# Two edits to the order of work in a hybrid attention and SSM block: the scaled x paced by weight units, and three small pieces of the scan put at one place

## The chip, the cores and the metric

The kernel runs on one core of a Trainium2 chip. The metric is the device time of one execution in microseconds (us). The kernel before took 1399.06 us, the median of three runs from 1398.83 to 1401.26.

A core has engines that run side by side, each with its own queue of instructions in a fixed order: TensorE (PE in the profile; its weight loads are PEld), VectorE (DVE), ScalarE (ACT), GpSimd (POOL) and SyncE (SP, which here only starts transfers). They wait for each other through semaphores. An instruction that waits holds up all that stands behind it on its engine.

## The reference

One layer of a block with 256 tokens and width 2048, all in fp32. What matters here:

```python
hn = rms_norm(x, norm_w)
proj = hn @ w_in                      # 2048 x 20544 columns
q, k, v, z_a, z_s, xbc, dt_raw, g_a, g_s = split(proj)
o_a = mixed_dilated_attention(q, k, v) * silu(z_a)
xs, bm, cm = split(silu(causal_depthwise_conv(xbc)))
dt = softplus(dt_raw + dt_bias); acum = cumsum(dt * a) within chunks of 128
cb = C @ B^T                          # per group and chunk
y = (cb * decay) @ (xs * dt) + carried state + d_skip * xs
y = rms_norm(y * silu(z_s), ssm_norm_w)
merged = sigmoid(g_a) * (o_a @ w_attn) + sigmoid(g_s) * (y @ w_ssm)
return rms_norm(x + merged @ w_out, final_norm_w)
```

The SSM part has 8 groups. A group has a block B and a block C of 128 columns and four blocks of 128 columns each of xs and z_s (8 heads of 64).

## The kernel before, in words

**Products in fp32.** Each operand of a product is kept as a high part h and a low part l, both of a shorter type that TensorE takes at a higher rate, and a product is three products (h by h, l by h, h by l). All weights are streamed once, in units of 128 partitions by 1024 numbers (`unit`, L210 to L222): SP starts the transfer of unit n into w, ScalarE writes h (L221) and VectorE writes l = w - h (L222). There are four buffers each for w, h and l, so unit n can be split once TensorE is done with unit n - 4. The units stand in one order for the whole kernel: first a mixed block (unit 0 to 7), dt (unit 8), the gates gs 0 and 1 (units 9 to 24), then the groups.

**The start.** The first block and the gates gs 0 and 1 are computed from x without its row norm, as split in yT[0], and the norm is multiplied in behind. All that follows takes x with the norm, kept split in XT. `find_r` (L717) computes the norm of each row and spreads it over the partitions: rb_x on TensorE (L481), and a copy rx on VectorE (L717) that lies in the tile `early`. `norm_x(c)`, for c from 0 to 7, takes two of the 16 blocks of x: one multiplication by rx over 128x512 (L530), and for each block the split, h on ScalarE (L229) and l on VectorE (L233). The first product that reads XT is xs of block 1, right behind the gates. Also waiting for rx are the first step of dt (L561), a multiplication of the three raw conv inputs (L606) and one of z_s (L721).

**A projection.** B, C, each xs and each zs are one projection each (`gemm_a`): 2 units, 32 matmuls, in turn one with h (128x512, L260) and one with l (128x256, L261).

**The SSM pieces of a group.** Beside its ten projections, a group g has three pieces on TensorE:

- C B (`make_cb`): two matmuls "cbp" (L617, L618) into a bank of PSUM called m1, then a multiplication by the mask on VectorE (L619).
- the turning of x (`turn`): eight transposes "xtp" (L650) into two banks m1, then two multiplications by dt on VectorE (L653). There are two m1 banks in all.
- the scan (`scan`): 32 matmuls "yp" (L668) of 64 columns each into the m2 banks, then on VectorE and ScalarE the work on y: L678, L681, the squares L682, the sums ssq L683, and the split into yT (L229, L233). Of the last group yT is needed by the product that follows the groups, ssm.

The scan needs `decays`: for each of four pairs of heads a transfer acb (256 KB, L626, one buffer) from acum, which dt has written to memory (L583), six ScalarE instructions (L631, L635), and per two pairs an exponential (L639) and a multiplication by C B on VectorE (L640). The bias of these comes from `dt_turn` (TensorE transposes dt_tp L591, and lastb L595).

**What sets the order.** Each projection calls `tick()` once, a gate product once per two units. `after(t, f)` puts f on a list to be written t ticks later. `on_unit[n]` is called when unit n has been split. This gives the order in which the program is written; from it a scheduler puts the instructions into the queues of the engines, with the splitting of units 120 places ahead.

Of the kernel before, what the change touches and what calls it, by code (L numbers as in the profile page):

```python
# [9 lines left out]
F32 = mybir.dt.float32  # L10
F32R = mybir.dt.float32r
AF = mybir.ActivationFunctionType
ALU = mybir.AluOpType
PSUM = bass.MemoryType.PSUM

P = 128
S = 256
# [4 lines left out]
SH = 64  # L22
# [10 lines left out]
X_CUTS = ((0, 1), (1, 2), (2, 4), (4, 6), (6, 8), (8, 10))  # L33
N_FINE = 4
N_ACT_X = 1
DT_LAG, CB_LAG, TURN_LAG, GT_LAG, Y_LAG, S_LAG, M_LAG = 2, 3, 2, 2, 11, 2, 2
GS_BEFORE = {0: (0, 1), 4: (2,)}
NEG = -1.0e30
S_QUADS = {
    ("ssm", 0): (5, 7, 9, 11, 13), ("ssm", 2): (3, 5, 7, 9, 11, 13),  # L40
# [14 lines left out]
def weight_plan():  # L55
# [5 lines left out]
    def rows(tag, src, off, n_kt):  # L61
        plan.append((tag, "b", src, off, n_kt, 512))
# [6 lines left out]
    for g in range(GROUPS):  # L69
        for c in GS_BEFORE.get(g, ()):  # L70
            rows(("gs", c), "w_in", OFF_GS + c * 512, KT)
# [78 lines left out]
def constants():  # L150
# [7 lines left out]
    count = m1.astype(np.float32) + m2 + m3  # L158
    cst[:, 0:384] = np.where(count > 0, -dist, NEG)
    cst[:, 384:768] = count  # L160
# [11 lines left out]
def hybrid_block(ctx: ExitStack, tc: tile.TileContext, wall, xt, x, pk_d, cst_d, fw_d, out):  # L172
    nc = tc.nc
    ve, ac, gp, pe = nc.vector, nc.scalar, nc.gpsimd, nc.tensor
# [29 lines left out]
    on_unit = {}  # L204
# [23 lines left out]
    def split(src, hi, lo, scale=1.0):  # L228
        ac.activation(hi, src, AF.Copy, scale=scale)  # L229
        if isinstance(scale, float):  # L230
            ve.tensor_tensor(lo, src, hi.bitcast(F32), ALU.subtract)
        else:
            ve.scalar_tensor_tensor(lo, src, scale, hi.bitcast(F32), ALU.mult, ALU.subtract)  # L233
# [4 lines left out]
    def after(ticks, f):  # L238
        due.append((now[0] + ticks, f))
# [78 lines left out]
    def half_silu(h, out_ap, name):  # L318
        th = ev.tile([P, S], F32, name=f"th_{name}", tag="th", bufs=2)
        ac.activation(th, h, AF.Tanh)  # L320
        ve.scalar_tensor_tensor(out_ap, th, 1.0, h, ALU.add, ALU.mult)
# [140 lines left out]
    def gates(tag, th, src, scales=(0.5, 0.5)):  # L462
        accs = gemm_b(tag, lambda kt: src[:, kt, :])
        for i in range(2):
            ac.activation(th[:, i, tag[1] * 512 : tag[1] * 512 + 512], accs[i], AF.Tanh, scale=scales[i])
# [20 lines left out]
    xr, dts, rx = early[:, :KT, :], early[:SH, KT:28, :], early[:, 28, :]  # L486
# [19 lines left out]
    def fetch(dst, src, behind):  # L506
        gp.tensor_copy(dst[:, 0:1], behind)
        nc.sync.dma_start(dst, src)
# [16 lines left out]
    on_unit[10] = lambda behind: fetch(cst[:, 1152:], cst_d[:, 1152:], behind)  # L525
    on_unit[13] = lambda behind: fetch(cst[:, :1152], cst_d[:, :1152], behind)

    def norm_x(c):
        cs = slice(2 * c, 2 * c + 2)
        ve.tensor_tensor(xr[:, cs], xr[:, cs], rx.unsqueeze(1).to_broadcast([P, 2, S]), ALU.mult)  # L530
        for kt in range(2 * c, 2 * c + 2):
            split(xr[:, kt], XT[:, kt, :S], XT[:, kt, S:], scale=pk[:, kt : kt + 1])

# [2 lines left out]
    with tc.tile_pool(name="ssm", bufs=2) as sp:  # L536
        ev = sp
        for tag in ("lo", "eh", "th"):
            sp.tile([P, S], F32, name=f"first_{tag}", tag=tag, bufs=2)
        dtT = sp.tile([P, 2, SH], F32, name="dtT", tag="dtT", bufs=1)  # L540
        acT = sp.tile([P, 2, SH], F32, name="acT", tag="acT", bufs=1)
        crT = sp.tile([P, SH], F32, name="crT", tag="crT", bufs=1)
# [10 lines left out]
        def dt_chain():  # L553
            used = []

            def tmp():
                used.append(0)
                return dts[:, len(used) - 1, :]

            raw, neg, e, z, s, pl, lo, dt, da, ac_t, one = (tmp() for _ in range(11))  # L560
            ve.tensor_tensor(raw, lo, rx[:SH], ALU.mult)  # L561
            ve.tensor_scalar(raw, raw, pk[:SH, 320:321], None, ALU.add)
            ve.scalar_tensor_tensor(neg, raw, -1.0, raw, ALU.mult, ALU.max)
            ac.activation(e, neg, AF.Exp, scale=-1.0)
            ve.tensor_scalar(s, e, 2.0, None, ALU.add)
            ve.reciprocal(z, s)
            ve.tensor_tensor(z, z, e, ALU.mult)
            ve.tensor_tensor(s, z, z, ALU.mult)
            ve.tensor_scalar(pl, s, 1.0 / 17.0, 1.0 / 15.0, ALU.mult, ALU.add)
            for n in (13, 11, 9, 7, 5, 3, 1):  # L570
                ve.tensor_tensor(pl, pl, s, ALU.mult)
                ve.tensor_scalar(pl, pl, 1.0 / n, None, ALU.add)
            ve.tensor_tensor(pl, pl, z, ALU.mult)
            ve.tensor_scalar(pl, pl, 2.0, None, ALU.mult)
            ve.tensor_scalar(raw, raw, 0.0, None, ALU.max)
            ve.tensor_tensor(dt, pl, raw, ALU.add)
            ac.activation(a_neg, pk[:SH, 321:322], AF.Exp)
            ve.tensor_scalar(da, dt, a_neg, -1.0, ALU.mult, ALU.mult)
            gp.memset(one, 1.0)
            for c in range(2):  # L580
                cs = slice(c * P, (c + 1) * P)
                ve.tensor_tensor_scan(ac_t[:, cs], one[:, cs], da[:, cs], 0.0, ALU.mult, ALU.add)
            nc.sync.dma_start(acum_d, ac_t)  # L583
            after(DT_LAG, lambda: dt_turn(dt, ac_t))

        def dt_turn(dt, ac_t):
            tp = bank("m1", 2, "dt_tp")
            for i, src in enumerate((dt, ac_t)):
                for c in range(2):
                    o = (2 * i + c) * SH  # L590
                    pe.transpose(tp[:, o : o + SH], src[:, c * P : (c + 1) * P], ident[:SH, :SH])  # L591
            ve.tensor_copy(dtT, tp[:, 0:128].rearrange("p (c h) -> p c h", c=2))
            ve.tensor_copy(acT, tp[:, 128:256].rearrange("p (c h) -> p c h", c=2))
            lastb = bank("m2", 2, "lastb")
            pe.matmul(lastb[:, :SH], sel, acT[:, 0], start=True, stop=True)  # L595
            ve.tensor_tensor(crT, lastb[:, :SH], acT[:, 0], ALU.subtract)
# [6 lines left out]

        def conv(raw, ct, out_ap, name, late=False):
            if late:
                ve.tensor_tensor(raw[:, 4:], raw[:, 4:], rx, ALU.mult)  # L606
            h = ev.tile([P, S], F32, name=f"cv_{name}", tag="eh", bufs=2)
            ac.activation(h, raw[:, 4:], AF.Identity, scale=cw[:, 144 + ct : 145 + ct], bias=cw[:, 192 + ct : 193 + ct])
            for k in range(3):
                ve.scalar_tensor_tensor(  # L610
                    h, raw[:, 1 + k : 1 + k + S], cw[:, 48 * k + ct : 48 * k + ct + 1], h, ALU.mult, ALU.add
                )
            half_silu(h, out_ap, name)

        def make_cb(g, bt, ct_, cb):
            p = bank("m1", 2, f"cbp{g}")
            pe.matmul(p[:, :S], bt[:, :P], ct_, start=True, stop=True)  # L617
            pe.matmul(p[:, S : S + P], bt[:, P:], ct_[:, P:], start=True, stop=True)  # L618
            ve.tensor_tensor(cb, p[:, :384], mask3, ALU.mult)  # L619
# [85 lines left out]
        zh0 = first["zs"][:, 0]  # L705
# [12 lines left out]
            ve.tensor_scalar(cw, pk[:, 16:256], 0.5, None, ALU.mult)  # L718

        def finish_z0():  # L720
            ve.tensor_tensor(zh0, zh0, rx, ALU.mult)  # L721
            half_silu(zh0, zh0, "z0")

        after(2, find_r)
        for c in range(8):
            after(3 + c * 6 // 8, lambda c=c: norm_x(c))
        for ticks, f in (
            (8, dt_chain),
            (9, lambda: conv(raws[0], 32, group[0], "B0", True)),
            (9, lambda: conv(raws[1], 40, group[1], "C0", True)),  # L730
            (10, lambda: conv(raws[2], 0, first["xs"][:, 0], "x0", True)),
            (10, finish_z0),
            (11, lambda: make_cb(0, *group)),
        ):
            after(ticks, f)
        for c in GS_BEFORE[0]:
            gates(("gs", c), th_s, yT[0], hr_x)

        for g in range(GROUPS):
            if g:  # L740
                for c in GS_BEFORE.get(g, ()):
                    gates(("gs", c), th_s, XT)
# [6 lines left out]
            for t in range(max(4 * g, 1), 4 * g + 4):  # L749
                u, i = divmod(t, 2)  # L750
# [3 lines left out]
                if t % 4 == 3:  # L754
                    after(TURN_LAG, lambda a=(g, state): turn(*a))

                    y_lag = Y_LAG + 4 * len(GS_BEFORE.get(g + 1, ()))
                    for k in range(4):
# [144 lines left out]
    with tc.tile_pool(name="fin", bufs=2) as fp:  # L903
# [40 lines left out]
        for c0 in (0, 2):  # L944
# [8 lines left out]
            for i in range(2):  # L953
                f = fs[:, i, :8]
                for c, acc in zip((c0, c0 + 1), es[2 * i : 2 * i + 2]):
                    cs = slice(c * 512, (c + 1) * 512)
# [11 lines left out]
        for i in range(2):  # L968
            r = fs[:, i, 7:8]
            for c in range(4):  # L970
                cs = slice(c * 512, (c + 1) * 512)
# [40 lines left out]
```

## Time and profile before

| | |
|---|---|
| median of three runs | 1399.06 us (1398.83 to 1401.26) |
| the profiled execution's own time | 1398.06 us |
| its span, first to last instruction | 1396.3 us |
| granted TensorE clock, mean | 0.998 |
| TensorE busy | 1383.9 us (99%) |
| VectorE busy | 1088.8 us (78%) |
| ScalarE busy | 810.2 us (58%) |
| GpSimd busy | 18.7 us (1%) |
| instructions | 19873 |
| memory traffic | 194 GB/s over the span |

The profiled execution is 1.0 us under the median, and 1.8 us of it lie outside the span. The trace models the end of a matmul and lets neighbours overlap, so the duration of a row is longer than the distance to the next; the time that a stretch of TensorE takes is read from the starts. All times in what follows are microseconds from the first instruction of the profiled execution.

### The profile page before, as it was taken

The page shows a single profiled execution, that of the slowest core. Times are in us where ns is not written, and L with a number is a line of the kernel's source. Part 1 is how long each engine was busy: PE and PEld are TensorE (multiplying, and loading weights), DVE is VectorE, ACT ScalarE, POOL GpSimd, SP SyncE. Part 2 cuts the span into 40 slices and gives each one's busy share as a digit, 9 for nine tenths or more (in the row PEclk, how much of TensorE's full clock was granted, in tenths as well). Part 3 has the DMA queues.
Part 4 walks back from the last instruction along what each step waited for, and adds up shares of the span by engine and source line. Part 5 has one row for each costly group of instructions (what it writes and reads, how often), then busy time and mean ns, then how long its engine had stood idle before and what let it go on. Part 6 is the DMA issues. An engine that isn't in the chain of part 4 may idle for free.

```text
span 1396.3 us, 19873 instructions
## 1 busy us (share of the span) xinstructions
PE 1383.9 (99%) x7308; PEld 1178.1 (84%) x7308; DVE 1088.8 (78%) x1622; ACT 810.2 (58%) x1258; POOL 18.7 (1%) x72
## 2 busy tenths in 40 slices
PE   9999999999999999999999999999999999999997
PEld 8788888888888888888888888888888888888886
DVE  6988787786788787798988988666666766487887
ACT  7657577675667575665554555545454454454554
POOL 1000000000000000000000000000000000000000
PEclk9999999999999999999999999999999999999999
DMA  8666665666565665556666565655555555667564
GB/s 333 217 205 207 184 204 170 213 183 205 175 204 180 208 188 185 181 175 212 190 221 196 193 215 183 211 179 170 176 169 180 176 172 172 204 211 245 175 199 136
DMA packets 78210, 272.33 MB, mean 195 GB/s; under 512 B 8800, under 2 KB 9376, under 8 KB 77728
## 3 DMA queue, kind: packets, MB, share of 16 engines
q1 hardware_dynamic: 77392, 269.88, 61.4%
q8 instruction: 57, 0.93, 0.3%
q10 hardware_dynamic: 720, 1.18, 0.2%
q14 instruction: 41, 0.34, 0.1%
HBM read 268.86 MB, written 2.16 MB: 194 GB/s over the span
## 4 chain that ended last, share of the span: by engine, by line
PE 97%; DVE 2%; DMA 0%; issue 0%; ACT 0%; SPq 0%; POOL 0%; POOLq 0%; DVEq 0%
PE ps_zs L260 8%; PE ps_xs L260 8%; PE ps_k L260 4%; PE ps_za L260 4%; PE ps_q L260 4%; PE ps_zs L261 4%; PE ps_xs L261 4%; PE ps_ssm L377 3%; PE ps_ssm L379 3%; PE ps_ssm L378 3%; PE ps_q L261 2%; PE ps_za L261 2%; PE ps_k L261 2%; PE ps_B L260 2%; PE ps_C L260 2%; PE ps_gs L337 2%
## 5 line engine op out<-in xcount | busy, mean ns | idle before, releaser
L222 DVE TENSOR_TENSOR l<-w,h 128x1024 fp32r<-128x1024 f32 (+1 forms) x432 | 522.0, 1212 | 222.7 <-ACT h L221 219.9
L221 ACT ACTIVATE h<-w 128x1024 fp32r<-128x1024 f32 (+1 forms) x432 | 452.0, 1050 | 417.1 <-issue 98.4
L260 PE MATMUL ps_zs<-XT,h 128*128 128x512 f32 x496 | 175.7, 396 | 0.0
L260 PE MATMUL ps_xs<-XT,h 128*128 128x512 f32 x496 | 174.5, 393 | 0.0
L261 PE MATMUL ps_zs<-XT,l 128*128 128x256 f32 x496 | 139.5, 281 | 0.0
L261 PE MATMUL ps_xs<-XT,l 128*128 128x256 f32 x496 | 139.1, 280 | 0.0
L260 PEld LDWEIGHTS ps_zs<-XT,h 128*128 128x128 f32 x496 | 93.0, 187 | 22.1 <-issue 1.2
L260 PEld LDWEIGHTS ps_xs<-XT,h 128*128 128x128 f32 x496 | 92.9, 187 | 20.9
L261 PEld LDWEIGHTS ps_zs<-XT,l 128*128 128x128 f32 x496 | 93.7, 189 | 0.1
L261 PEld LDWEIGHTS ps_xs<-XT,l 128*128 128x128 f32 x496 | 93.7, 189 | 0.0
L260 PE MATMUL ps_q<-XT,h 128*128 128x512 f32 x256 | 92.4, 404 | 0.0
L260 PE MATMUL ps_za<-XT,h 128*128 128x512 f32 x256 | 89.7, 394 | 0.0
L260 PE MATMUL ps_k<-XT,h 128*128 128x512 f32 x256 | 89.7, 394 | 0.0
L261 PE MATMUL ps_q<-XT,l 128*128 128x256 f32 x256 | 71.3, 278 | 0.0
L261 PE MATMUL ps_k<-XT,l 128*128 128x256 f32 x256 | 71.0, 278 | 0.0
L261 PE MATMUL ps_za<-XT,l 128*128 128x256 f32 x256 | 71.0, 278 | 0.0
L378 PE MATMUL ps_ssm<-l,yT 128*128 128x512 f32 x168 | 65.2, 389 | 0.0
L379 PE MATMUL ps_ssm<-h,yT 128*128 128x512 f32 x168 | 65.2, 390 | 0.0
L377 PE MATMUL ps_ssm<-h,yT 128*128 128x512 f32 x168 | 57.5, 390 | 0.0
L260 PEld LDWEIGHTS ps_k<-XT,h 128*128 128x128 f32 x256 | 48.0, 188 | 11.3
L260 PEld LDWEIGHTS ps_za<-XT,h 128*128 128x128 f32 x256 | 48.0, 188 | 11.3
L260 PEld LDWEIGHTS ps_q<-XT,h 128*128 128x128 f32 x256 | 48.1, 188 | 10.9
(517 smaller groups left out, 2963.7 us busy)
## 6 DMA issues: line engine op xcount, KB each, us to landing
w<-in_wall SPq DMA_DIRECT2D x480, 512.0 KB, 3.7
acb<-acum_d SPq DMA_DIRECT2D x32, 256.0 KB, 3.6
th_s<-in_x SPq DMA_DIRECT2D x4, 512.0 KB, 7.1
vth<-in_x SPq DMA_DIRECT2D x1, 2048.0 KB, 9.4
early<-in_xt SPq DMA_DIRECT2D x7, 256.0 KB, 6.8
fw<-in_fw SPq DMA_DIRECT2D x1, 1024.0 KB, 6.0
out<-vth SPq DMA_DIRECT2D x4, 256.0 KB, 2.9
out<-vth ACTq DMA_DIRECT2D x4, 256.0 KB, 3.2
```

The source lines that it names most:

```text
L221: ac.activation(h[:, a:b], w[:, a:b], AF.Copy)
L222: ve.tensor_tensor(l[:, a:b], w[:, a:b], h[:, a:b].bitcast(F32), ALU.subtract)
L260: pe.matmul(acc, h[:, kk, :], m, start=(kt == 0), stop=False)
L261: pe.matmul(acc[:, S:], l[:, kk, :], m[:, :S], start=False, stop=(kt == KT - 1))
L337: pe.matmul(accs[i], xh, l[:, kk], start=False, stop=False)
L377: pe.matmul(acc, xh, h, start=start, stop=False)
L378: pe.matmul(acc, xh, l, start=False, stop=False)
L379: pe.matmul(acc, xl, h, start=False, stop=stop)
```

## The change

**Scaled x.** `norm_x(0)` still takes rx itself, three ticks on. For c from 1 to 7, `norm_x(c)` is now written when unit 16 + c has been split (units 17 to 23, one block each). Ahead of it GpSimd makes a copy of rx for this c, in a new tile rxs that shares the memory of the tile gt: it first copies one column of the unit's h into the place (128x1), which makes it wait for that unit, and then rx (128x256). The multiplication of `norm_x(c)` reads that copy, and so waits for the unit. The other readers of rx (dt, the raw conv inputs, z_s) read the last copy, and dt is due one tick later.

**SSM pieces.** The lags of the list change, in ticks: C B from 3 to 9.5, the turning of x from 2 to 3, decays from 2 to 3, the scan from 11 to 13. A group has ten ticks; with these numbers the C B of group g, the scan of group g - 1 and the turning of x of group g are due at the same place, between B and C of group g + 1.

The number of instructions on TensorE, VectorE and ScalarE is the same but for the grouping; GpSimd has 14 more.

```diff
-DT_LAG, CB_LAG, TURN_LAG, GT_LAG, Y_LAG, S_LAG, M_LAG = 2, 3, 2, 2, 11, 2, 2
+DT_LAG, CB_LAG, TURN_LAG, GT_LAG, Y_LAG, S_LAG, M_LAG = 2, 9.5, 3, 3, 13, 2, 2
 GS_BEFORE = {0: (0, 1), 4: (2,)}
+RX_UNITS = {c: 16 + c for c in range(1, 8)}
...
+    rx_of = {}
+
+    def later_rx(n):
+        def copy(behind):
+            rx_of[n] = rxs[:, n]
+            gp.tensor_copy(rx_of[n][:, 0:1], behind)
+            gp.tensor_copy(rx_of[n], rx)
+        return copy
+
     def norm_x(c):
         cs = slice(2 * c, 2 * c + 2)
-        ve.tensor_tensor(xr[:, cs], xr[:, cs], rx.unsqueeze(1).to_broadcast([P, 2, S]), ALU.mult)
+        r = rx_of.get(c, rx)
+        ve.tensor_tensor(xr[:, cs], xr[:, cs], r.unsqueeze(1).to_broadcast([P, 2, S]), ALU.mult)
...
+        rxs = sp.tile([P, 12, S], F32, name="rxs", tag="gt", bufs=1)
...
-            ve.tensor_tensor(raw, lo, rx[:SH], ALU.mult)
+            ve.tensor_tensor(raw, lo, rx_of[7][:SH], ALU.mult)
...
-                ve.tensor_tensor(raw[:, 4:], raw[:, 4:], rx, ALU.mult)
+                ve.tensor_tensor(raw[:, 4:], raw[:, 4:], rx_of[7], ALU.mult)
...
-            ve.tensor_tensor(zh0, zh0, rx, ALU.mult)
+            ve.tensor_tensor(zh0, zh0, rx_of[7], ALU.mult)
...
-        for c in range(8):
-            after(3 + c * 6 // 8, lambda c=c: norm_x(c))
+        after(3, lambda: norm_x(0))
+        for c, u in RX_UNITS.items():
+            on_unit[u] = lambda behind, c=c: (later_rx(c)(behind), norm_x(c))
         for ticks, f in (
-            (8, dt_chain),
+            (9, dt_chain),
```

Below, rows of the queues as the two programs have them: line, operation, result <- operands, with the number of the unit or block in the name, and x for the same row several times. The lines of the changed program are 1 to 14 higher than those of the kernel before.

VectorE at the start, before. The first row is the copy rx, "early" on the left of a TENSOR_TENSOR of 128x512 is a `norm_x` multiplication, XT the l part of a split block of x, l16 to l18 the l parts of the weight units of gs 1.

```order
L717 COPY early_80<-rb_x_450 128x256
L530 TENSOR_TENSOR early_80<-early_80 128x512 x8
L561 TENSOR_TENSOR early_80<-early_80 64x256
L606 TENSOR_TENSOR raw_first0_348<-raw_first0_348,early_80 128x256
L606 TENSOR_TENSOR raw_first1_353<-raw_first1_353,early_80 128x256
L606 TENSOR_TENSOR raw_first2_358<-raw_first2_358,early_80 128x256
L721 TENSOR_TENSOR zs0_364<-zs0_364,early_80 128x256
L222 TENSOR_TENSOR l16_565<-w16_562,h16_564 128x1024
L233 SCALAR_TENSOR_TENSOR XT_77<-early_80,pk_72,XT_77 128x256 x8
L222 TENSOR_TENSOR l17_592<-w17_589,h17_591 128x1024
```

The same place after:

```order
L730 COPY early_80<-rb_x_451 128x256
L542 TENSOR_TENSOR early_80<-early_80 128x512
L223 TENSOR_TENSOR l16_556<-w16_553,h16_555 128x1024
L234 SCALAR_TENSOR_TENSOR XT_77<-early_80,pk_72,XT_77 128x256 x2
L223 TENSOR_TENSOR l17_578<-w17_575,h17_577 128x1024
L542 TENSOR_TENSOR early_80<-early_80,rxs_114 128x512
L223 TENSOR_TENSOR l18_603<-w18_600,h18_602 128x1024
```

One multiplication, not eight, stands ahead of l16; the others follow one to a unit, each behind the l of its unit, and the multiplications for dt, the raw inputs and z_s stand behind l23.

TensorE in a steady group, before: the scan of group 1 (yp1) between an xs and a zs, then the transposes of group 2 (xtp2) four matmuls ahead of the end of B of group 3, then C B of group 3 (cbp3) inside a zs.

```order
L668 MATMUL yp1_0_2385<-gt1_1836,xdt1_1823 64x128 x2
L260 MATMUL ps_zs11_2423<-XT_77,h75_2426 128x512
...
L261 MATMUL ps_B3_2500<-XT_77,l78_2526 128x256
L650 MATMUL xtp2_1_2480<-cst_78,xs5_2250 128x128 x4
L650 MATMUL xtp2_0_2479<-cst_78,xs4_2024 128x128 x4
L260 MATMUL ps_B3_2500<-XT_77,h78_2525 128x512
...
L617 MATMUL cbp3_2746<-ct3_2476,bt3_2475 128x256
L618 MATMUL cbp3_2746<-ct3_2476,bt3_2475 128x128
L261 MATMUL ps_zs13_2808<-XT_77,l87_2812 128x256
```

After, between B and C of group 3 (the rows of yp1 that repeat left out):

```order
L262 MATMUL ps_B3_2451<-XT_77,l78_2477 128x256
L630 MATMUL cbp2_2509<-ct2_1794,bt2_1793 128x256
L631 MATMUL cbp2_2509<-ct2_1794,bt2_1793 128x128
L681 MATMUL yp1_1_2514<-gt1_1909,xdt1_1896 64x256 x2
L681 MATMUL yp1_1_2514<-gt1_1909,xdt1_1896 64x128 x2
...
L681 MATMUL yp1_0_2513<-gt1_1909,xdt1_1896 64x128 x2
L663 MATMUL xtp2_1_2553<-cst_78,xs5_2261 128x128 x4
L663 MATMUL xtp2_0_2552<-cst_78,xs4_2031 128x128 x4
L261 MATMUL ps_C3_2573<-XT_77,h79_2576 128x512
```

All three pieces stand in one row, and a matmul with h follows.

TensorE at the end of the groups, before: the scan of group 7 (yp7) begins inside the last gate product, gs 3, is broken by ten of its matmuls, and ends ahead of ssm.

```order
L668 MATMUL yp7_1_6098<-gt7_5914,xdt7_5901 64x256
L337 MATMUL ps_gs3_0_5899<-l192_6070,XT_77 128x512
L338 MATMUL ps_gs3_0_5899<-h192_6069,XT_77 128x512
```

After, inside ssm:

```order
L380 MATMUL ps_ssm0_3_6216<-h195_6255,yT0_81 128x512
L681 MATMUL yp7_1_6113<-gt7_5965,xdt7_5952 64x256 x2
L681 MATMUL yp7_1_6113<-gt7_5965,xdt7_5952 64x128 x2
...
L681 MATMUL yp7_0_6112<-gt7_5965,xdt7_5952 64x128 x2
L378 MATMUL ps_ssm0_0_6213<-h196_6261,yT0_81 128x512
```

The scan of group 7 is whole again and stands 36 matmuls into ssm.

## The prediction

> **What bounds the kernel now.** I read the page first, then the waits of TensorE, the chain, and the timeline where the change works. The page:
>
> ```profile
> PE 1383.9 (99%) x7308; PEld 1178.1 (84%) x7308; DVE 1088.8 (78%) x1622; ACT 810.2 (58%) x1258; POOL 18.7 (1%) x72
> ...
> PE 97%; DVE 2%; DMA 0%; issue 0%; ACT 0%; SPq 0%; POOL 0%; POOLq 0%; DVEq 0%
> ```
>
> TensorE is busy for 99% of the span and holds 97% of the chain; 2% belongs to VectorE. So the change can gain in two ways only: a wait of TensorE goes, or the same matmuls run in less time. The waits:
>
> ```profile
> PE ps_gs L337 <- DVE l L222: 1.7, 2, 1.2
> PE warm L492 <- DVE ssq L489: 1.4, 1, 1.4
> PE ps_first L306 <- ACT h L221: 0.2, 1, 0.2
> ```
>
> Only the first lies where the change works: two waits of the gate product for an l. The chain shows what is late there (start, duration):
>
> ```profile
> 43.67 0.76 DVE early L530 x2
> 44.43 0.45 issue
> 44.88 3.70 DVE early L530 x6
> ...
> 50.25 1.14 DVE l L222
> 51.38 2.05 DVE XT L233 x6
> ...
> 54.56 1.13 DVE l L222
> ...
> 58.73 1.15 DVE l L222
> 59.92 0.50 PE ps_gs L337
> 62.49 0.45 PE ps_gs L336 x2
> 65.21 0.45 PE ps_gs L336 x2
> ```
>
> From 43.67 on VectorE does the eight multiplications of norm_x in one go (0.62 each), and splits of x ahead of l17 and l18, for which TensorE then waits. The last two rows are one weight unit apart: 2.72 us. In the timeline the two late matmuls stand as
>
> ```profile
> 55.75 0.50 PE L337 MATMUL ps_gs<-l,yT 128*128 128x512 f32 x1 [0.55 <-DVE l L222]
> 59.92 0.50 PE L337 MATMUL ps_gs<-l,yT 128*128 128x512 f32 x1 [1.15 <-DVE l L222]
> ```
>
> 0.55 + 1.15 = 1.7 us of waiting. Behind each wait TensorE also has to start up again, so by the starts of all matmuls there the two cost about 2.0 us.
>
> **Scaled x: what it removes.** With one multiplication ahead of l16, VectorE's run is 0.62 (norm_x 0), 1.14 (l16), two splits 0.68 (2.05 / 6 each), 1.14 (l17) from 43.67: l17 is there at 47.3, where the first of the two waits shows that it is wanted at 55.2. Lead 7.9 us. Each further unit then asks VectorE for 1.14 + 0.68 + 0.62 = 2.44 us against 2.72 of TensorE. Ahead of l24 also stand the multiplications for dt, the raw inputs and z_s, 1.7 us (the chain's gap between the last norm_x, 48.58, and l16, 50.25). So both stalls go: **-2.0 us**, unless the copies cost what the next paragraph bounds. It cannot be more, since TensorE waits for nothing else there.
>
> **Scaled x: what it adds.** Seven copies of 128x1 and seven of 128x256 on GpSimd, and a wait of seven multiplications for them. No 128x256 copy on GpSimd is in the trace. The nearest rows are one-column copies:
>
> ```profile
> 29.74 1.24 POOL L507 COPY cst<-h 128x1 f32<-128x1 f32 x1 [3.25 <-ACT h L221]
> 38.90 0.18 POOL L507 COPY cst<-h 128x1 f32<-128x1 f32 x1 [0.30 <-ACT h L221]
> ```
>
> The same copy takes 0.18 or 1.24 us. The long one starts with an l of VectorE, which the same h releases, and lasts as long as that l does. So a GpSimd copy can be held by a VectorE instruction; whether VectorE is held too these rows do not say. Per unit, what the multiplication waits, w, lies between 0 (the first copy hides beside the l, the second beside the two splits) and 2.48 (both take 1.24, nothing hides them). Slack of l24: 7.9 + 7 x (2.72 - 2.44) - 1.7 - 7w = 8.2 - 7w, and never more than some 4.7, since h23 can be written only when unit 19 has been used. VectorE stalls TensorE again from w = 1.2. I take w = 0.3 (a short second copy that falls between two splits), and **+0.3 us** for what ScalarE, which has the same splits to do, may be late with; ends 0 and 9.2 (7 x 2.48 - 8.2).
>
> A page of the Trainium skill speaks against the change here. "SBUF — State Buffer", section "Who interferes with whom", says that VectorE and GpSimd share a pair of ports as an exclusive lock, that an instruction of VectorE with two operands in SBUF contends with a GpSimd instruction that reads SBUF, and that the loser is blocked for the whole instruction. The trace agrees with the half that it shows (1.24 against 0.18 us); that VectorE loses as well no row shows.
>
> The last rx copy now comes behind unit 23, so dt starts some 20 us later, and its result too. The first C B, decays and dt_turn of group 0 follow. Group 0 has its transposes at 123 before and at nearly the same matmul after, so its four decays, each behind its transfer,
>
> ```profile
> acb<-acum_d SPq DMA_DIRECT2D x32, 256.0 KB, 3.6
> ```
>
> fall into about 25 us in which ScalarE also writes the h of nine units. The scan of group 0, which needs them, stands 13 ticks on and gives room. An h that is queued behind a decay that waits for its transfer could be late: 0 to 2.5 us (a transfer of 3.6 less about one unit of the projections' lead); I take **+0.4**, near the low end, because the transfers overlap with other groups' work in every later group without a wait.
>
> **SSM pieces: pace.** A projection of 32 matmuls takes one of two times. Starts of two whole projections, each row the first matmul of one, the second pair behind a C B:
>
> ```profile
> 131.72 0.40 PE L260 MATMUL ps_zs<-XT,h 128*128 128x512 f32 x1
> ...
> 137.38 0.40 PE L260 MATMUL ps_xs<-XT,h 128*128 128x512 f32 x1
> ...
> 143.65 0.39 PE L260 MATMUL ps_zs<-XT,h 128*128 128x512 f32 x1
> ...
> 149.19 0.39 PE L260 MATMUL ps_xs<-XT,h 128*128 128x512 f32 x1
> ```
>
> 5.66 against 5.54 us. By the starts of all projections, the slower pace begins behind a scan or a gate product, and ends behind transposes or a C B that stand ahead of the right matmul: behind xtp ahead of an h it always ended. Counted, the slower pace holds for 27.6 projections (4 at the start, 3.2 in group 0, 12 around group 4, 1.9 behind each of four other scans, 1 at the end). After the change xtp stands right behind the scan and ahead of an h of C, so I expect it for 18.2 only (7.2 at the start, since the transposes that end it come with the later dt, and 11 behind the gates of group 4): 9.4 x 0.11 = **-1.0 us**. Ends: no change of pace, 0; or all 76 projections slow, +5.3.
>
> **SSM pieces: fewer breaks.** The pieces of one steady group, each with the row behind it, and the distance to the next scan:
>
> ```profile
> 226.08 2.82 PE L668 MATMUL yp<-gt,xdt 128*64 128x256 f32 x32
> ...
> 228.83 0.50 PE L260 MATMUL ps_zs<-XT,h 128*128 128x512 f32 x1
> ...
> 239.54 1.04 PE L650 MATMUL xtp<-cst,xs 128*128 128x128 f32 x8
> ...
> 240.33 0.48 PE L260 MATMUL ps_B<-XT,h 128*128 128x512 f32 x1
> ...
> 264.57 0.59 PE L617 MATMUL cbp<-ct,bt 128*128 128x256 f32 x2
> ...
> 265.14 0.36 PE L261 MATMUL ps_zs<-XT,l 128*128 128x256 f32 x1
> ```
> ```profile
> 226.15 2.75 PE yp L668 x32
> ...
> 286.30 2.75 PE yp L668 x32
> ```
>
> 2.75 + 0.79 + 0.57 = 4.11 us for the pieces, ten projections at 5.54 are 55.4, and the group takes 60.15: 0.64 are left. 1.9 slow projections are 0.2 of it; the rest, 0.4 to 0.45, is the cost of going into and out of three places. In the attention part three such pieces stand in one row already:
>
> ```profile
> 1002.55 0.59 PE L875 MATMUL ops<-pT,vth 128*128 128x256 f32 x2
> ...
> 1004.00 0.58 PE L260 MATMUL ps_q<-XT,h 128*128 128x512 f32 x1
> 1004.42 0.28 PE L261 MATMUL ps_q<-XT,l 128*128 128x256 f32 x1
> 1004.54 0.40 PE L260 MATMUL ps_q<-XT,h 128*128 128x512 f32 x1
> ```
>
> There the first pair behind takes 0.54 where a pair takes 0.35, and nothing is lost ahead: about 0.2 for one place. One place instead of three saves 0 to 0.4 a group; I take 0.15, since the scan, with tiles of 64 columns, still stands between pieces of 128: 7 places x 0.15 = **-1.05 us** (ends 0 and -2.9).
>
> "TensorEngine Tiling (Array Packing)" of the Trainium skill, section "Key Properties", says that a change of the tiling mode drains TensorE. By that rule the scan's two edges stay, whatever stands beside it, and only the edges of the other pieces are saved, which is the lower half of these ends.
>
> At the end of the groups the scan of group 7 is now whole. Before, two of its matmuls ran alone:
>
> ```profile
> 578.62 0.65 PE L668 MATMUL yp<-gt,xdt 128*64 128x256 f32 x2
> 579.20 0.50 PE L337 MATMUL ps_gs<-l,XT 128*128 128x512 f32 x1
> ```
>
> 0.58 for two where 32 take 2.75: **-0.5 us**.
>
> **SSM pieces: who waits.** C B, scan and xtp need three banks m1 and there are two: the second half of xtp waits until VectorE has done the mask of C B. The scan of 2.75 us between them covers that (0.5 us of work, first in VectorE's queue there); if VectorE were 3 us late, it would cost the excess. Behind the place VectorE has y, xdt and the squares together, about 7 us in which an l is queued; units of projections are 2.77 us apart and four buffers ahead, so I cost it at nothing. Not so at the end: y of group 7 comes some 11 us later, into the stretch where VectorE is the fuller engine:
>
> ```profile
> 560.00:605.00 45.00, 45.00 (x223) 36.55 (x222) 34.75 (x51) 30.39 (x46) 0.70 (x1) 1.00 0.57 186
> 605.00:646.00 41.00, 41.00 (x182) 33.96 (x181) 39.42 (x58) 25.02 (x33) 0.00 (x0) 1.00 0.56 180
> ```
>
> Behind the length of the stretch stand the busy times of PE, PEld, DVE, ACT and POOL: DVE has 34.75 of 45 us before 605 and 39.42 of 41 behind it. Work of 6.2 us (y, sums, splits) partly moves over that border: VectorE has 1.6 us of spare time there, and TensorE no wait. I take **+0.4**, ends 0 and 4.
>
> **The sum.** -2.0 + 0.3 + 0.4 - 1.0 - 1.05 - 0.5 + 0.4 = -3.45 us against the profiled execution's 1398.06, so 1394.6; the median of the runs shown is 1.0 higher, and I forecast 1399.06 - 3.45 = 1395.6. 0.2% is 2.8 us, about what a measurement of this kernel can tell from no change.
>
> **Rivals.**
> - The copies hold VectorE. One mechanism, at units 17 to 23: each multiplication waits w for two copies that are themselves held. For: 1.24 against 0.18 above, and VectorE is nearly full there (2.44 of 2.72). Against: the first copy lies beside an l that must end anyway. Stall 7w - 8.2: it makes up for the other terms (-3.75 without the copies' 0.3) from w = 1.7 on, and ends slower than 1401.9 from w = 2.1; at 2.48 it is 1404.5. The lock of the Trainium skill's page "SBUF — State Buffer" would give this end if VectorE lost about as often as GpSimd. Chance 0.13, of which 0.08 slower.
> - The pace does not follow xtp but the scan, or the matmul that the place is put ahead of: all projections slow, 1395.6 + 1.0 + 5.3 = 1401.9. For: it begins behind every scan. Against: behind xtp ahead of an h it ended five times of five in the groups. Chance 0.07, of which 0.04 slower.
> - VectorE's late y at the end of the groups and the late decays of group 0 cost their upper ends: +6.5 - 0.8, 1401.3; with half of that 1398. Chance 0.20, of which 0.04 slower, where part of the copies' stall is added.
> - The place saves all edges, and the pace is fast behind group 4's place too: -1.85 - 1.2 more, 1392.6. Chance 0.10.
> - The forecast, 1393.8 to 1397.2: chance 0.50, some four fifths of it under 1396.3.
>
> Faster by over 0.2%: 0.40 + 0.10 = 0.50. Slower: 0.08 + 0.04 + 0.04 = 0.16. Between: 0.34. The range 1392.6 to 1402.3 leaves 0.05 under it and about 0.13 over it; the likeliest case alone reaches from 1393.8 to 1397.2.
>
> **What would show it.** Right: no wait of ps_gs for l in the waits of TensorE; the 128x256 copies under 1.3 us; the distance from scan to scan in a steady group near 59.8, not 60.15, with C and all behind it at 5.54; the scan of group 7 in one piece. Wrong: a wait of ps_gs or of the first xs for l or XT between 60 and 80 (the copies); projections at 5.66 behind the place (the pace); a wait of ps_ssm for an l behind 600, or of a projection for h between 110 and 145 (late work of VectorE and ScalarE).

## The result

The changed kernel takes 1402.97 us (median of 12 runs, 1402.16 to 1404.08) against 1399.20 us of the kernel before on the same chips (12 runs, 1398.24 to 1401.26): ratio 1.0026, 95% interval 1.0018 to 1.0034. It is slower by 3.8 us; 1395.6 had been forecast, with a range up to 1402.3.

The page of the changed kernel, its engines and the chain:

```profile
PE 1388.2 (99%) x7308; PEld 1178.6 (84%) x7308; DVE 1088.4 (78%) x1622; ACT 808.1 (58%) x1258; POOL 31.2 (2%) x86
...
PE 96%; DMA 1%; DVE 1%; ACT 1%; issue 0%; SPq 0%; POOL 0%; POOLq 0%; DVEq 0%; ACTq 0%
```

The waits of its TensorE:

```profile
PE ps_first L307 <- ACT h L222: 1.9, 2, 1.4
PE warm L493 <- DVE ssq L490: 1.4, 1, 1.4
PE ps_ssm L378 <- ACT htu L419: 0.6, 1, 0.6
```

The wait of gs 1 is gone, as forecast. TensorE is busy 4 us longer with the same 7308 matmuls. Adding up the distances between the starts of its matmuls, by what they compute (us in each profiled execution):

| | before | after | difference |
|---|---|---|---|
| first block | 24.0 | 25.5 | +1.5 |
| gates gs 0 to 3 | 90.2 | 87.4 | -2.7 |
| projections xs, zs, B, C | 427.3 | 430.8 | +3.5 |
| pieces cbp, yp, xtp, dt_tp, lastb | 34.3 | 35.4 | +1.1 |
| ssm | 166.9 | 168.5 | +1.6 |
| all that follows | | | below 0.2 |

The first block belongs to no part of the change: in the profiled executions of the kernels below, which are alike up to there, its end lies anywhere from 32.4 to 34.0 us. Without it the rest is +3.5, close to the 3.8 of the runs.

The projections tell the story. First matmuls of three projections in a row of group 3, where the kernel before has 5.54 us from one to the next:

```profile
247.95 0.40 PE L261 MATMUL ps_xs<-XT,h 128*128 128x512 f32 x1
...
253.60 0.40 PE L261 MATMUL ps_zs<-XT,h 128*128 128x512 f32 x1
...
259.26 0.40 PE L261 MATMUL ps_xs<-XT,h 128*128 128x512 f32 x1
```

5.65 and 5.66 us: the slower pace. By the starts, all 76 projections of the changed kernel run at it. The distance from scan to scan, in the chain, is 60.97 where it was 60.15:

```profile
177.72 2.75 PE yp L681 x32
...
238.69 2.75 PE yp L681 x32
```

### The profile page after: what moved, and what is told of

Its sections match the earlier page's. It is cut to its first block, busy times and chain, and to the rows that moved or that the text cites. A ratio compares the mean times of both kernels' runs of the same rounds, so it can differ in the third digit from the quotient of the medians.

```text
span 1401.5 us, 19895 instructions
## 1 busy us (share of the span) xinstructions
PE 1388.2 (99%) x7308; PEld 1178.6 (84%) x7308; DVE 1088.4 (78%) x1622; ACT 808.1 (58%) x1258; POOL 31.2 (2%) x86
## 4 chain that ended last, share of the span: by engine, by line
PE 96%; DMA 1%; DVE 1%; ACT 1%; issue 0%; SPq 0%; POOL 0%; POOLq 0%; DVEq 0%; ACTq 0%
PE ps_zs L261 8%; PE ps_xs L261 8%; PE ps_k L261 4%; PE ps_za L261 4%; PE ps_q L261 4%; PE ps_xs L262 4%; PE ps_zs L262 4%; PE ps_ssm L380 3%; PE ps_ssm L379 3%; PE ps_ssm L378 3%; PE ps_q L262 2%; PE ps_za L262 2%; PE ps_k L262 2%; PE ps_gs L337 2%; PE ps_gs L339 2%; PE ps_gs L338 2%
```

## The experiments

"Fast" and "slow" below are the two paces of a projection, 5.55 and 5.65 us. The pace behind a piece was read from the starts of the matmuls. "The place of group g" is where C B and the transposes of group g stand, in the changed kernel with the scan of group g - 1; a place is entered or left at the pace of the matmuls ahead of it or behind it.

**Which half costs?** The two halves of the change alone.

```diff
 # changed kernel, lags of the kernel before
-DT_LAG, CB_LAG, TURN_LAG, GT_LAG, Y_LAG, S_LAG, M_LAG = 2, 9.5, 3, 3, 13, 2, 2
+DT_LAG, CB_LAG, TURN_LAG, GT_LAG, Y_LAG, S_LAG, M_LAG = 2, 3, 2, 2, 11, 2, 2
```

> The scaled x paced by units alone; the five lags as before the change. Theory (pace): the two waits of gs 1 go, projections keep the pace that they had before in groups 1 to 7, so about 2 us faster than before, 1397; TensorE's projections behind the transposes of each group at 5.55 us. Rival (the paced x itself costs: copies on GpSimd, dt 20 us later): slower than before, 1401 or more, with projections at 5.65 us or waits between 60 and 150 us.

Measured 1397.45 us (10 runs) against 1399.00: ratio 0.9989, 0.9980 to 0.9998.

```diff
 # kernel before, lags of the change
-DT_LAG, CB_LAG, TURN_LAG, GT_LAG, Y_LAG, S_LAG, M_LAG = 2, 3, 2, 2, 11, 2, 2
+DT_LAG, CB_LAG, TURN_LAG, GT_LAG, Y_LAG, S_LAG, M_LAG = 2, 9.5, 3, 3, 13, 2, 2
```

> The five lags alone; the scaled x as before. Theory (pace): the waits of gs 1 stay (1.7 us), all projections run at 5.65 us, so some 5 to 6 us slower than before, 1404 to 1405. Rival (paced x costs): no slower than before, 1399 or less.

Measured 1404.51 us: ratio 1.0038, 1.0024 to 1.0052. The scaled x gains 1.6 us, the lags lose 5.5, together 3.9: the halves add up to the whole. With the lags alone every projection behind 124 us is slow.

**Do single transposes end the slow pace?**

```diff
-... CB_LAG, TURN_LAG, GT_LAG, Y_LAG ... = ... 9.5, 3, 3, 13 ...
+... CB_LAG, TURN_LAG, GT_LAG, Y_LAG ... = ... 9.5, 4, 3, 13 ...
```

> The changed kernel with the transposes of x one projection later (lag 4 for 3): C B and scan between B and C, transposes between C and the first xs. If transposes that stand alone ahead of an h end the slow pace, as in the kernel before, only C of each group is slow, and 8 of 10 projections of some 7 groups gain 0.1 us each: 1398 to 1399. If the slow pace comes from the gates at the start and a scan keeps it whatever follows: 1403 to 1404.

Measured 1398.51 us (ratio 0.9994, 0.9984 to 1.0004): 4.3 us less than the changed kernel, each taken against the kernel before on its own chips, by one projection's delay of the eight transposes of each group. Slow are the projections up to 125 us, C of each group, and group 4 behind its gates; the projections behind the transposes are fast.

**Does it hang on the matmul that follows the place?** The place behind the first h of C instead of ahead of it.

```diff
-        tick()
+        inside = tag[0] == "C"
+        if not inside:
+            tick()
...
                 pe.matmul(acc, h[:, kk, :], m, start=(kt == 0), stop=False)
+                if inside and kt == 0:
+                    tick()
```

> The changed kernel with the whole place one matmul later: behind the first matmul of C, which has h, and so ahead of one with l. If the pace hangs on the matmul that follows the place, it can change to 5.55 us: 1397 to 1398. If it hangs on the pieces alone: 5.65 us as in the changed kernel, 1403.

Measured 1400.79 us, between the two. The same place (that of group g stands in C of group g + 1) left slow in groups 1, 4 and 6 and fast in groups 2 and 5; that of group 6 had been entered fast, the others slow. So the matmul behind it does not decide alone.

**Which neighbour keeps the pace slow?** Four variants with C B back at its old lag of 3, so that the place has the scan and the transposes only.

```diff
 # one pair between: transposes wait in a list, and are written behind the first l of C
+                while kt == 0 and held:
+                    held.pop(0)()
...
-                    after(TURN_LAG, lambda a=(g, state): turn(*a))
+                    if g in (3, 7):
+                        after(TURN_LAG, lambda a=(g, state): turn(*a))
+                    else:
+                        after(TURN_LAG, lambda a=(g, state): held.append(lambda: turn(*a)))
```

> The changed kernel with C B at its old lag of 3, and the transposes of a group one pair of matmuls later: scan, one h and one l of C, transposes, the rest of C. Theory (transposes end the slow pace only where a projection's l stands right ahead of them, not a scan): C and all behind it at 5.55 us, slow only for one pair a group; faster than the scaled x alone by what B and a zs ran slow there, about 1396.5. Rival (the pace is set by the whole sequence of times, whatever stands beside the transposes; or the scan and the transposes must be a projection apart): 5.65 us, 1402 or more.

Measured 1397.64 us: fast behind the transposes, as expected, but for group 0, where they touch the two lastb, and group 3, where they stand in the gates. The time is 1.1 us over the expectation; TensorE takes 1.6 us longer over ssm than before, as in the changed kernel (below).

> The changed kernel with C B at its old lag of 3 and nothing else: scan and transposes touch, C B stands alone inside a later projection. Theory (scan right ahead of the transposes keeps the slow pace): slow behind the place; a C B ahead of an l may end it, as in group 0 of the kernel before, in which case part of each group is fast: 1399 to 1402. Rival (it is C B in the place that keeps the pace slow): 5.55 us from C on, 1397.

Measured 1399.99 us, inside what the theory gave, but not for its reason: a C B ahead of an l made the pace fast at 142 us, as said, and then the touching scan and transposes left it fast, in groups 1, 2, 5 and 6. Only in group 4, entered slow behind the gates, did they leave it slow. A scan right ahead of the transposes does not make the pace slow.

```diff
 # touching, and one more matmul
+        if tag[0] == "C":
+            pe.matmul(acc[:, :P], ident, ident, start=True, stop=True)
```

> As the run with C B at lag 3, scan and transposes touching, but with one more matmul (fp32, 128x128, into C's own bank, which C's first matmul then writes over; it has no part in the result) between the transposes and the first h of C. If the pace depends on what stands next to the h, or on the time at which C begins, it can change to 5.55 us: 1398. If on the scan right ahead of the transposes alone: slow as without it.

Measured 1400.97 us, with fast and slow groups mixed. Scan, transposes and the extra matmul left the pace as they found it: slow in groups 2, 4 and 6, fast in groups 1 and 5.

```diff
 # one h between
                 pe.matmul(acc, h[:, kk, :], m, start=(kt == 0), stop=False)
+                while kt == 0 and held:
+                    held.pop(0)()
```

> As the run with one pair between, but with only the first h of C between scan and transposes, so that an h stands ahead of the transposes and an l behind. In the kernel before, the one place with transposes so (group 0, at 123 us) went from the fast pace to the slow one. Theory: slow behind the place, 1401 or more. Rival (any matmul of a projection between is enough): as with the pair, 1396.5.

Measured 1397.94 us, fast behind the place: the rival was right, and the one place of the kernel before (group 0, transposes ahead of an l) was no rule.

**Does the place make the pace slow, or does it only fail to end it?** So far the three pieces together had been entered slow. Here they are entered fast.

```diff
-                    after(TURN_LAG, lambda a=(g, state): turn(*a))
+                    after(TURN_LAG + (g in (0, 4)), lambda a=(g, state): turn(*a))
```

> The changed kernel, but in groups 0 and 4 alone the transposes one projection later (between C and xs, where the run with lag 4 showed that they end the slow pace). The place with all three pieces is so entered at the fast pace in groups 1, 2, 5 and 6. Theory (the three touching pieces leave the pace as it is, and the changed kernel is slow because nothing in it ends the slow pace of the gates): all projections between 125 and 293 us and from the xs of group 5 on at 5.55 us, some 56 projections by 0.1, 1397 to 1398. Rival (the three pieces make the pace slow, as a scan alone does): fast only up to the next place, some 18 projections, 1401.

Measured 1399.33 us (ratio 1.0002, 0.9993 to 1.0011): between theory and rival. The place of group 1 was entered fast and left slow; those of groups 5 and 6 were entered fast and left fast. First h of xs and of zs behind the place of group 1:

```profile
184.81 0.40 PE L261 MATMUL ps_xs<-XT,h 128*128 128x512 f32 x1
...
190.46 0.40 PE L261 MATMUL ps_zs<-XT,h 128*128 128x512 f32 x1
```

5.65 us. Same instructions at the place, two outcomes. But the two were not entered alike, though both at 5.55 us. The last two pairs ahead of the place of group 1, and then of group 5:

```profile
174.03 0.39 PE L261 MATMUL ps_B<-XT,h 128*128 128x512 f32 x1
174.26 0.28 PE L262 MATMUL ps_B<-XT,l 128*128 128x256 f32 x1
174.38 0.39 PE L261 MATMUL ps_B<-XT,h 128*128 128x512 f32 x1
174.61 0.28 PE L262 MATMUL ps_B<-XT,l 128*128 128x256 f32 x1
...
438.77 0.39 PE L261 MATMUL ps_B<-XT,h 128*128 128x512 f32 x1
439.00 0.27 PE L262 MATMUL ps_B<-XT,l 128*128 128x256 f32 x1
439.11 0.40 PE L261 MATMUL ps_B<-XT,h 128*128 128x512 f32 x1
439.34 0.28 PE L262 MATMUL ps_B<-XT,l 128*128 128x256 f32 x1
```

Ahead of group 1 all pairs are equal, 346 or 347 ns; ahead of group 5 a short pair and a long one take turns, 344 and 350 ns, with the same mean. Call the two fast patterns "equal" and "alternating". The next two kernels are this one with a single extra matmul some 22 us ahead of the place of group 1, 128 columns in the one and 256 in the other, into a bank that is written over.

```diff
+        if tag == ("zs", 6):
+            pe.matmul(acc[:, :P], ident, ident, start=True, stop=True)
```

> The run that entered the first place fast and left it slow (groups 0 and 4 a projection later), with one more fp32 matmul 128x128 ahead of the second zs of group 1 (into the bank that the zs then writes over; no part in the result), some 23 us ahead of that place. Nothing beside the place changes, only the time at which it is entered. If the pace behind the place hangs on that time: it may stay at 5.55 us behind the place at 179 us. If it hangs on the instructions beside the place: 5.65 us, as without the extra matmul.

> As the last run with a 128x256 matmul in place of the 128x128 one: another shift in time. Same question, same readings.

In both the pace is fast behind the extra matmul as it was ahead of it, but its pattern has changed: equal up to the extra matmul, alternating behind it and still so ahead of the place. With 128 columns:

```profile
174.65 0.39 PE L263 MATMUL ps_B<-XT,h 128*128 128x512 f32 x1
174.88 0.27 PE L264 MATMUL ps_B<-XT,l 128*128 128x256 f32 x1
174.99 0.40 PE L263 MATMUL ps_B<-XT,h 128*128 128x512 f32 x1
175.22 0.28 PE L264 MATMUL ps_B<-XT,l 128*128 128x256 f32 x1
```

Now the place of group 1 leaves fast, and so does the next. The first h of xs and of zs behind it:

```profile
185.32 0.39 PE L263 MATMUL ps_xs<-XT,h 128*128 128x512 f32 x1
...
190.87 0.39 PE L263 MATMUL ps_zs<-XT,h 128*128 128x512 f32 x1
```

5.55 us. One timed execution each: 1397.51 and 1397.77 us, below all ten without the extra matmul (1398.46 to 1400.24). Over all runs, the three pieces ahead of an h were entered in the alternating pattern 14 times and left it so 14 times; they were entered in the equal pattern twice (this place, and the same one in a later run) and left slow twice; and they were entered slow 17 times and left slow 17 times. So what comes behind the place goes with the pattern in which it is entered, and the same instructions can do either. The extra matmul shifts the time as well as the pattern; the pattern accounts for all 33 cases, and why it matters no run shows.

**The end of the groups.** The scan of group 6 two ticks earlier, so that decays and scan of group 7 come ahead of ssm again.

```diff
-                    y_lag = Y_LAG + 4 * len(GS_BEFORE.get(g + 1, ()))
+                    y_lag = Y_LAG + 4 * len(GS_BEFORE.get(g + 1, ())) - 2 * (g >= 6)
...
-                        after(GT_LAG + k if k < 3 else y_lag - 2, lambda a=(g, k, cb, state): decays(*a))
+                        after(GT_LAG - (g == 7) + k if k < 3 else y_lag - 2, lambda a=(g, k, cb, state): decays(*a))
```

> The changed kernel with the end of the groups as before: the scan of group 6 two ticks earlier, inside its own projections, so that decays of group 7 and its scan come ahead of ssm. Theory: the waits of ssm and of the quads for VectorE and ScalarE (1.4 us more than before between the start of ssm and attention) go, the pace stays slow up to group 6: 1401 to 1402. Rival (those waits have to do with something else than the late scan of group 7): 1403.

Measured 1401.26 us, 1.5 less than the changed kernel, each taken against the kernel before on its own chips, and the wait of ssm is gone from TensorE's waits. In the changed kernel it stands in the timeline as

```profile
660.65 0.50 PE L378 MATMUL ps_ssm<-htu,yT 128*128 128x512 f32 x1 [0.58 <-ACT htu L419]
```

and the stretch in which VectorE is full as

```profile
605.00:651.00 46.00, 45.86 (x206) 37.55 (x206) 43.65 (x67) 29.75 (x35) 1.48 (x1) 1.00 0.55 174
```

VectorE busy 43.65 of 46.00 us here, TensorE 45.86, and by the starts TensorE takes 1.6 us longer over ssm than before.

**Versions that gain.** Transposes of groups 0 and 4 a projection later and the end as before:

> The last two together: transposes of groups 0 and 4 a projection later, and the scan of group 6 early. Theory: both gains add up, 1396 to 1396.5, faster than both kernels. Rival of the first run (the place makes the pace slow): 1399.5 to 1400.

Measured 1397.51 us, ratio 0.9987 (0.9978 to 0.9996), between theory and rival, since the place of group 1 leaves slow here too.

The pair between, with transposes of group 0 a projection later, those of group 3 held up to C of group 4, and the end as before:

> The run with one pair between scan and transposes and C B at lag 3, with transposes of group 0 a projection later, those of group 3 held up to C of group 4, and the end of the groups as before. Theory: fast pace from 125 us on but for the gates and B of group 4, and no late work at ssm: 0.2 + 1.0 + 1.4 less than with the pair alone, 1395 to 1395.5. Rival (the gains of the pace do not show at the end, because other engines hold TensorE up): 1397 or more.

Measured 1397.59 us (ratio 0.9991, 0.9982 to 1.0000), 2 us over the expectation: the scheduler put the transposes of group 3 into the first pair of B of group 4, three ahead of its l and five behind, and group 4 stayed slow; and it moved the C B of group 1 ahead of an h, behind which the pace went from fast to slow.

Then the transposes of groups 0, 1, 2 and 4 a projection later, the end as before:

```diff
-                    after(TURN_LAG, lambda a=(g, state): turn(*a))
+                    after(TURN_LAG + (g in (0, 1, 2, 4)), lambda a=(g, state): turn(*a))
```

> The run with both (transposes of groups 0 and 4 a projection later, scan of group 6 early), and the transposes of groups 1 and 2 a projection later as well. If transposes alone between C and xs end the slow pace every time: only C of groups 2 and 3 is slow before the gates of group 4, 16 projections by 0.1 us less than with both, 1395.8 to 1396.2. Rival (pace in the profile gained, time not, since VectorE or ScalarE limits): 1397.5.

Measured 1395.96 us (11 runs, 1395.01 to 1396.99) against 1398.87: ratio 0.9977, 0.9968 to 0.9986, as expected and 0.2% faster than the kernel before. Behind the transposes between C and xs of group 2, first matmuls of xs, zs and the next xs:

```profile
184.66 0.60 PE L663 MATMUL xtp<-cst,xs 128*128 128x128 f32 x4
185.01 0.48 PE L261 MATMUL ps_xs<-XT,h 128*128 128x512 f32 x1
...
190.65 0.39 PE L261 MATMUL ps_zs<-XT,h 128*128 128x512 f32 x1
...
196.20 0.39 PE L261 MATMUL ps_xs<-XT,h 128*128 128x512 f32 x1
```

5.64 us with the longer first pair, then 5.55.

## Why the prediction was wrong

- **What bounds the kernel.** Right: TensorE, and the only wait within reach was that of gs 1.
- **The stall of gs 1, -2.0.** Right. The 192 matmuls of gs 0 and 1 take 43.6 us by the starts where they took 45.9: -2.3. The half alone gains less, 1.6 us, because the later dt moves the piece that first ended the slow pace from 97 us to 142 us, some four slow projections more, and dt_tp is broken into three.
- **The copies, +0.3, ends 0 and 9.2.** The cost was nothing, at the lower end. Rows of GpSimd at the units 17, 18 and 21, and of VectorE's first paced multiplication:

```profile
49.31 1.24 POOL L535 COPY rxs<-h 128x1 f32<-128x1 f32 x1 [9.13 <-ACT h L222]
50.61 0.40 POOL L536 COPY rxs<-early 128x256 f32<-128x256 f32 x1
...
53.33 0.55 POOL L536 COPY rxs<-early 128x256 f32<-128x256 f32 x1
...
60.55 1.29 POOL L536 COPY rxs<-early 128x256 f32<-128x256 f32 x1
```
```profile
51.05 0.69 DVE L542 TENSOR_TENSOR early<-early,rxs 128x512 f32<-128x512 f32 x1 [0.54 <-POOL rxs L536]
...
53.15 1.02 DVE L234 SCALAR_TENSOR_TENSOR XT<-early,pk,XT 128x256 fp32r<-128x256 f32 x2
...
60.37 1.22 DVE L223 TENSOR_TENSOR l<-w,h 128x1024 fp32r<-128x1024 f32 x1
```

The wide copy takes 0.40 us alone, 0.55 beside splits, and 1.29 when an l of VectorE has started 0.18 us ahead of it. The longest wait of a multiplication was 0.54 us, the others 0.3 or none, under the 1.2 from which TensorE would have waited by the prediction (with its own cap of 4.7 on the lead, some 0.7). The rule of the Trainium skill's page "SBUF — State Buffer", section "Who interferes with whom" (the later of the two is blocked until the first has ended), agrees with the long rows. VectorE lost at most 0.15 us: its two splits beside the copy at 53.33 take 1.02 where others take 0.87.
- **Late decays of group 0, +0.4.** Nothing: TensorE waits for no h there.
- **Pace, -1.0. This is the step that failed.** It read: "behind xtp ahead of an h it always ended". That was true of all five cases, and of 24 more in these runs, but in every one of them the transposes stood alone behind an l of a projection. The change put them behind a scan, for which there was no case; and at the start it put those of group 0 right behind the two lastb (120.4 us), where they left the pace slow too, as they did in six other runs. Entered at the slow pace, the three pieces together ahead of an h left it slow 17 times of 17 in these runs; entered fast they left it fast 14 times of 16, every time but in the equal pattern. The changed kernel enters the first one slow from the gates, has taken away the lone C B and the lone transposes that used to end that pace, and so stays slow to the end: some 49 more slow projections at 0.106, +5.2 us. It is the second rival, which had been given 0.07 and 1401.9 us; its mechanism too was only half right, since neither the scan nor the place sets the pace for good.
- **Fewer breaks, -1.05.** A third of it. With the place entered and left fast, two such places are 59.9 us apart (C begins behind them at 442.4 and 502.3 us in the run with 128 extra columns); before it was 60.15, of which 0.2 are slow projections. That is 0.05 for each place, about 0.4 in all. The pieces touch, but C B and transposes then take longer themselves: C B 0.75 for 0.57, xtp 0.85 for 0.79.
- **Scan of group 7 whole, -0.5.** It runs in one piece of 2.75; about right.
- **Late y at the end, +0.4, ends 0 and 4.** The place was right, the size was not: +1.6 us over ssm by the starts, and 1.5 less in the runs when it was undone.

The sum with measured terms: -2.3 + 5.2 + 0.2 (dt_tp in more pieces) - 0.4 - 0.5 + 1.6 = +3.8, against 3.8 of the runs and 3.5 by the starts; agreement to better than 0.3 us is chance. In the prediction's arithmetic, the items of its 27.6 slow projections add up to 27.8, and 7 places at 0.4 to 2.8, not 2.9; neither moves the forecast.

## What to carry to other kernels

Where one engine is busy for 99%, a change of order acts through the pace of that engine's instructions as much as through waits: look at the distance between starts of the same instruction in different stretches, not only at waits and busy shares, and at the single distances as well as their mean. A rule read from a handful of cases holds for the neighbours that those cases had; where the change makes a new neighbourhood, both outcomes belong in the sum, priced for all the work behind it. If such a pace can be reset by a piece that is there anyway, place that piece early, and one at a time.

## What the runs showed of the hardware

Two paces of the same sequence were seen, matmuls of 512 and 256 columns in turn with new weights for each: 346.7 ns a pair, or 353.3 ns, at a granted clock of 1.00 in both. The slow one has a pattern that repeats every three pairs (361, 349 and 350 ns); the fast one comes in two patterns, equal pairs of 346 to 347 ns or pairs of 344 and 350 ns in turn. A stretch keeps its pace until something else comes between; one h of the next projection put between an h and its l was enough (524 us in the run with the place one matmul later: slow to fast).

What came behind a piece went with the piece, its neighbours, and the pattern ahead of it:

- Lone transposes behind an l and ahead of an h ended the slow pace 29 times of 29.
- A C B alone behind an h and ahead of an l left equal pairs every time (32 times), whatever came ahead.
- A scan alone, or C B and scan, ahead of an h: entered slow, it left the pace slow; entered in equal pairs, it made the pace slow every time; entered in alternating pairs, the scan alone left it fast twice, and C B with the scan made it slow once.
- Stretches of gates were followed by the slow pace except in the run with an extra matmul there.

Which pattern a piece leaves, and what in the engine it is that goes in or out of step, stays open: no run here shows it.
